# A layer with memory attention on one core: products of high and low parts for the memory's keys and values, and the keys' projection ahead of the last trunk stage

## Chip, core and metric

The kernel runs on one core of one Trainium2 chip. The metric is the device time of one execution in microseconds, the median of several runs. TensorE (PE) multiplies matrices, VectorE (DVE) and ScalarE (ACT) work on tiles, GpSimd (POOL) takes some copies, and SyncE (SP) issues the DMAs between memory and the core.

## What is computed

One layer on 2048 positions of width 1024: a mixer (dilated window attention beside a gated convolution), a cross-attention into 256 fixed memory tokens, and an MLP. Everything is float32. What the change touches is the cross-attention:

```python
def memory_cross_attention(h, mem_n, w_q_mem, w_kv_mem, w_o_mem):
    q = (h @ w_q_mem).reshape(b, s, N_MEM_HEADS, MEM_HEAD_DIM)
    kv = mem_n @ w_kv_mem
    k, v = jnp.split(kv, 2, axis=-1)
    ...
    scores = jnp.einsum('bshe,bmhe->bhsm', q, k).astype(jnp.float32) / math.sqrt(MEM_HEAD_DIM)
    p = jax.nn.softmax(scores, axis=-1).astype(v.dtype)
    o = jnp.einsum('bhsm,bmhe->bshe', p, v).reshape(b, s, D_MODEL)
    return o @ w_o_mem

x = x + hybrid_mixer(rms_norm(x, g_mix), ...)
x = x + memory_cross_attention(rms_norm(x, g_xattn), rms_norm(mem, g_mem), ...)
x = x + squared_relu_mlp(rms_norm(x, g_mlp), w_up, w_down)
return rms_norm(x, g_final)
```

The memory does not depend on x, so the kernel folds it into the weights: the keys K = mem_n @ w_k are multiplied once with w_q (per head, 256 columns), and the values V with w_o. The 2048 positions then need one product with the folded query weights and one with the folded output weights.

## The kernel before

All products of the trunk run on TensorE in *groups* of 28 *steps*. A step multiplies one tile of weights with one tile of data and is numbered through (group times 28); `step(n)` issues its products, `ahead` prepares operands of a later one, `behind` and `done` take the results out of PSUM. Groups come in this order: two groups each of "vg", "ux" and "qk" (the mixer's projection, the last one, "qk" for the second half, is steps 84 to 111), then the dilated attention, then "w" (the mixer's output projection), "s" and "o" (scores and outputs of the memory), and the MLP.

The trunk's float32 products are already taken of high and low parts: an operand x is split into hi = x rounded to the reduced type float32r (ScalarE, L205 for weights, L298 for data) and lo = x - hi (VectorE, L212 and L309), and hi·hi + hi·lo + lo·hi is accumulated in PSUM (L416, 512 columns; L411, 256 columns). The memory's four sets of products are not: `mem_proj` (L1060) for keys and values, `fold_q` (L1043) for w_q times the keys and `fold_o` (L1331) for the values times w_o are plain float32 matmuls, of 128x256, 128x256 and 128x512. Each set goes over eight weight tiles of 128x1024.

Between step 111 and the attention stands a loop of 16 turns: eight of `mem_proj` (keys, into K5), then eight of `fold_q`. In it SP is told to load the first queries (`load_q`) and keys (`load_k`, L762), VectorE copies the keys to the second 64 partitions (`dup_k`, the cast at L769), and the first two score products (`qk`, L827 and L828) stand ahead of the last `fold_q`. The last convolution block, conv(0, 0), is spread over these turns too (scaled copies on ScalarE, taps at L680 and L681 on VectorE, row sums L114 on TensorE).

The attention repeats scores, softmax, transposes and products, and its tail combines three patterns (`combine`: sums at L927 to L939 on VectorE over rows that go out to memory and back). Its end is followed by a loop of 16 turns: `mem_proj` for the values and `fold_o`, beside which the combined attention is normalised and the operands of "w" are made.

The order is written by hand: each engine executes its instructions in the order in which the program issues them, `after(n, fn)` issues fn at step n, and `later(d, fn)` d turns after the current one. An instruction that waits holds all that stand behind it on its engine. Buffers are rings: 20 pages of 128x2048 floats (`page`), six smaller ones (`w4`), eight of `s2`, eight PSUM banks; taking the next buffer makes its writer wait for the last reader of the one that had it. `Weights` loads tiles in pairs, seven ahead. DMAs from SP take eight queues in turn.

Of the kernel before, what the change touches and what calls it, by code (L numbers as in the profile page):

```python
# [50 lines left out]
def _body(tc, a, out):  # L51
# [75 lines left out]
    class Weights:  # L127
        def __init__(self, srcs):
            self.srcs, self.raw = srcs, {}
# [10 lines left out]

        def get(self, i):
            for d in range(7):
                self.load(i + d)
            return self.raw[i]
# [544 lines left out]
    for (hf, j), ds in {(0, 1): (60, 63, 66, 70), (1, 0): (85, 88, 91, 94), (1, 1): (103, 105, 107, 109),  # L689
                        (0, 0): (117, 118, 119, 121)}.items():  # L690
# [9 lines left out]
    def mk(k):  # L700
        return mem["x"][:, k]

# [16 lines left out]
    WS2 = Weights([a["w_kv"][i] for i in range(8)] + [a["w_qT"][i] for i in range(8)])  # L719
    for n, fn, *args in ((32, mem_load, a["memT"]), (40, mem_rows), (94, mem_load, memd),  # L720
                         (98, WS2.load, 0), (106, WS2.load, 2), (109, WS2.load, 4)):
        after(n, fn, *args)
    for k in range(2):
        after(34 + 2 * k, mem_sum, k)
    for k in range(KC):
        after(41 + k, mem_scale, k)
    for n in range(V0 - 4, V0):
        ahead(n)
    for n in range(V0, 4 * 28):
        step(n, n > V0)  # L730
# [299 lines left out]
    A = {}  # L1030
    K5 = page([128, KC, J])

    def fold_q(t):
# [6 lines left out]
        w = WS2.get(8 + t)  # L1040
        for fc in range(KC):
            ps = bk["f"][fc // 2][:, fc % 2 * J:fc % 2 * J + J]
            pe.matmul(ps, w[:, fc], K5[:, t], start=e == 0 and fc % 2 == 0, stop=e == 1, skip_group_check=True)  # L1043
# [13 lines left out]
    def mem_proj(t, w, KV):  # L1057
        ps = bank()[:, :J]
        for k in range(KC):
            pe.matmul(ps, w[:, k], mk(k), start=k == 0, stop=k == KC - 1)  # L1060
        act.activation(KV[:, t], ps, AF.Copy)

    for j in range(16):
        if j < 8:
            mem_proj(j, WS2.get(j), K5)
        else:
            if j == 15:
                act.activation(dummy, ones, AF.Exp)
                qk(0)
                qk(1)  # L1070
            fold_q(j - 8)
        behind(4 * 28 + j)
        if j == 4:
            load_q(0)
        if j == 10:
            load_v(0, 2)
        if j in (6, 7, 8, 9):
            load_k(0, (j - 6) // 2, (j - 6) % 2)
        if j in (10, 11, 12, 13):
            dup_k(0, (j - 10) // 2, (j - 10) % 2, dve)  # L1080
# [3 lines left out]
    for i in range(len(units) + 4):  # L1084
# [7 lines left out]
        if i == 192 - 40:  # L1092
# [8 lines left out]
            later(43, WS.load, 6)  # L1101
        tick()
# [213 lines left out]
    V5 = page([128, KC, J])  # L1316

    def fold_o(t):
# [7 lines left out]
        for jb in range(2):  # L1326
            jl = slice(jb * 128, jb * 128 + 128)
            for nh in range(2):
                ns = slice(nh * 4, nh * 4 + 4)
                ps = bk["f"][jb][nh]  # L1330
                pe.matmul(ps, V5[:, t, jl], w[:, ns], start=e == 0, stop=e == 1)  # L1331
# [176 lines left out]
```

## Time and profile before

| | us |
|---|---|
| median of 3 runs (2668.38 to 2672.39) | 2671.26 |
| the profiled execution | 2672.2 |
| its span, first to last instruction | 2670.4 |
| TensorE busy in it | 2622.3 |
| VectorE busy | 2188.5 |
| ScalarE busy | 1443.3 |
| step 111 ends, the keys' products begin | 509.07 |
| the fold of the keys begins | 538.49 |
| the attention's scores run on from | 579.49 |
| the values' products begin | 853.18 |
| the fold of the values begins | 881.68 |
| stage "w" begins | 911.29 |

The upper rows are of the whole execution, the lower ones are start times in its timeline, on TensorE. A row of the timeline has start, duration, engine, line, operation and tiles; in square brackets stands the idle time of the engine before it and what ended that. A row of groups by line has the busy time of the whole group, the mean of one in ns, and idle time. A row of windows has for its stretch the busy time of PE, PEld, DVE, ACT and POOL (with counts), then the granted TensorE clock, the DMA share and GB/s.

### The profile page before, as it was taken

How to read it: one execution, taken by the hardware profiler on the slowest of the kernel's cores; microseconds unless marked ns; L12 is line 12 of the kernel's file. 1: busy time of each engine (PE TensorE's matmuls, PEld its weight loads, DVE VectorE, ACT ScalarE, POOL GpSimd, SP SyncE). 2: the span in 40 equal slices, each digit the busy share in tenths (PEclk: the TensorE clock that was granted, in tenths of full speed). 3: DMA queues.
4: the chain of work that ended last, by engine and by line, in shares of the span. 5: the costliest groups of instructions: out<-in, count | busy, mean ns of one | idle time of the engine just before them, and what ended most of it. 6: DMA issues, size and time to landing. Idle time of an engine off the chain costs nothing.

```text
span 2670.4 us, 35198 instructions
## 1 busy us (share of the span) xinstructions
PE 2622.3 (98%) x13286; PEld 2158.6 (81%) x13286; DVE 2188.5 (82%) x3405; ACT 1443.3 (54%) x2450; POOL 144.1 (5%) x181
## 2 busy tenths in 40 slices
PE   8999999989999999999999999999999999999998
PEld 6787988878888678888888888888887888888886
DVE  6879868658777689888999877879789987978788
ACT  5445545458776234667445546474644637365563
POOL 0000000002654200000000000000000000000000
PEclk9999999999999999999999999999999999999999
DMA  5856664994778866565683211111120511111111
GB/s 191 278 178 203 213 215 154 315 250 104 162 161 250 256 224 230 186 207 228 232 299 117 85 48 64 63 63 64 63 95 32 189 63 63 64 34 57 52 48 63
DMA packets 201673, 391.67 MB, mean 147 GB/s; under 512 B 21664, under 2 KB 77344, under 8 KB 188064
## 3 DMA queue, kind: packets, MB, share of 16 engines
q1 hardware_dynamic: 200960, 388.90, 45.0%
q8 instruction: 105, 1.72, 0.3%
q14 instruction: 64, 0.52, 0.1%
q10 hardware_dynamic: 544, 0.52, 0.1%
HBM read 277.12 MB, written 112.26 MB: 146 GB/s over the span
## 4 chain that ended last, share of the span: by engine, by line
PE 81%; DVE 9%; DMA 6%; ACT 2%; issue 1%; POOL 1%; SPq 1%; DVEq 0%; POOLq 0%; ACTq 0%
PE ps L416 65%; PE ps L884 3%; PE ps L867 2%; PE ps L433 2%; PE ps L827 2%; PE ps L411 1%; DMA pg<-qkd 1%; PE ps L828 1%; DVE pg L309 1%; DVE w L212 1%; PE ps L114 1%; DMA bgd<-pg 1%; PE ps L1060 1%; PE ps L1331 1%; POOL pg L954 1%
## 5 line engine op out<-in xcount | busy, mean ns | idle before, releaser
L416 PE MATMUL ps<-pg,w 128*128 128x512 f32 x8844 | 2033.3, 391 | 10.7 <-DVE pg L309 4.9
L416 PEld LDWEIGHTS ps<-pg,w 128*128 128x128 f32 x8844 | 1655.1, 188 | 359.8 <-DVE pg L309 10.5
L205 ACT ACTIVATE w<-pg 128x1024 fp32r<-128x1024 f32 x288 | 303.4, 1053 | 283.1 <-PE ps L416 237.6
L212 DVE TENSOR_TENSOR w<-pg,w 128x1024 fp32r<-128x1024 f32 x288 | 351.8, 1222 | 57.0 <-ACT w L205 56.4
L309 DVE TENSOR_TENSOR pg<-pg 128x1024 fp32r<-128x1024 f32 x300 | 365.0, 1217 | 5.0 <-ACT pg L298 4.6
L298 ACT ACTIVATE pg<-pg 128x1024 fp32r<-128x1024 f32 x300 | 305.8, 1046 | 29.2 <-DVE pg L264 11.3
L850 ACT ACTIVATE s<-s,stat 128x256 f32<-128x256 f32 (+1 forms) x384 | 172.6, 451 | 48.8 <-DVE stat L839 47.3
L1249 DVE TENSOR_TENSOR pg<-ps,pg 128x512 f32<-128x512 f32 x223 | 152.2, 685 | 53.6 <-PE ps L416 50.5
L445 ACT ACTIVATE s<-pg 128x1024 f32<-128x1024 f32 x79 | 83.3, 1057 | 187.1 <-DVE pg L1126 105.2
L205 ACT ACTIVATE w<-s 128x1024 fp32r<-128x1024 f32 x92 | 96.9, 1053 | 123.4 <-PE ps L416 74.7
L839 DVE CUSTOM_DVE_ANT_0 s<-ps,w 128x256 f32<-128x256 f32 (+1 forms) x344 | 109.0, 371 | 32.3 <-PE ps L828 27.1
L1220 DVE TENSOR_TENSOR pg<-ps,pg 128x512 f32<-128x512 f32 x96 | 66.0, 688 | 77.6 <-PE ps L416 77.6
L264 DVE TENSOR_TENSOR pg<-pg 128x1024 f32<-128x1024 f32 x104 | 126.7, 1218 | 1.5 <-DMA pg<-ptd 0.6
L212 DVE TENSOR_TENSOR w<-s,w 128x1024 fp32r<-128x1024 f32 x92 | 111.9, 1217 | 2.5 <-ACT w L205 2.4
L827 PE MATMUL ps<-pg 128*128 128x256 f32 x384 | 108.0, 313 | 0.7 <-DVE pg L769 0.7
L870 DVE COPY s<-ps 128x256 f32<-128x256 f32 (+1 forms) x192 | 101.0, 567 | 8.7 <-ACT s L850 8.0
L1215 ACT ACTIVATE pg<-ps 128x512 f32<-128x512 f32 x96 | 56.9, 595 | 90.2 <-PE ps L416 89.6
L1221 ACT ACTIVATE pg<-pg 128x512 f32<-128x512 f32 x96 | 60.6, 631 | 80.9 <-DVE pg L1220 80.8
L309 DVE TENSOR_TENSOR pg<-s,pg 128x1024 fp32r<-128x1024 f32 x78 | 94.5, 1220 | 9.7 <-ACT pg L298 9.6
L828 PE MATMUL ps<-pg 128*128 128x256 f32 x384 | 98.2, 287 | 3.7 <-DVE pg L769 3.7
L39 DVE TENSOR_TENSOR s<-s,s 128x1024 f32<-128x1024 f32 x56 | 69.2, 1236 | 31.5 <-ACT s L445 31.5
L867 PE MATMUL ps<-ident,s 128*128 128x128 f32 x600 | 86.4, 279 | 8.8 <-ACT s L850 8.3
(159 smaller groups left out, 2484.4 us busy)
## 6 DMA issues: line engine op xcount, KB each, us to landing
pg<-w_up SPq DMA_DIRECT2D x32, 1024.0 KB
pg<-w_down SPq DMA_DIRECT2D x32, 1024.0 KB
pg<-smd SPq DMA_DIRECT2D x24, 1024.0 KB
pg<-xT SPq DMA_DIRECT2D x19, 1024.0 KB
pg<-w_in SPq DMA_DIRECT2D x18, 1024.0 KB
qkd<-pg SPq DMA_DIRECT2D x64, 256.0 KB
pg<-qkd SPq DMA_DIRECT2D x32, 512.0 KB
pg<-x2d SPq DMA_DIRECT2D x16, 1024.0 KB
```

The costliest lines, as they stand in the source:

```text
L205: act.activation(hi, src, AF.Copy)
L212: dve.tensor_tensor(lo, src, f(hi), OP.subtract)
L264: dve.tensor_tensor(to, x, y, op)
L298: act.activation(hi, src, AF.Copy)
L309: dve.tensor_tensor(lo, src, f(hi), OP.subtract)
L416: pe.matmul(ps, wt[l][:, m % 2, k * 128:k * 128 + 128], o[x][:, k, cols], start=k == 0 and j == 0 and p in (1, 2, 5), stop=k == 3 and j == ...
L827: pe.matmul(Sh, qv, kv[0], start=True, stop=False)
L828: pe.matmul(Sh, qv, kv[1], start=False, stop=True)
L839: dve.tensor_tensor_reduce(smv, sv, mv, -0.125, 3e38, OP.add, OP.min, mt[:, c1:c1 + 1])
L850: act.activation(pout, pin, AF.Exp, bias=mt[:, c1:c1 + 1], scale=-1.0, accum_out=zt[:, c1:c1 + 1])
L867: pe.transpose(pt[:, j * 256 + h * 128:j * 256 + h * 128 + 128], PR[i][:, h * 256 + half * 128:h * 256 + half * 128 + 128], ident)
L1249: dve.tensor_tensor(y, ps, y, OP.add)
```

## The change

`Weights` gets a method `split` that makes a high and a low part of a tile, in two halves of a page or (pages=False) in two `w4` buffers; `get` splits one tile ahead and returns the pair. The memory is split the same way in four instructions (`mem_split`). The keys and values are taken from PSUM as a high copy (ScalarE) and a low part (VectorE). Every product of `mem_proj`, `fold_q` and `fold_o` becomes three, of PARTS. The keys' projection goes out of the loop behind step 111 to a place between steps 83 and 84, with its loads at steps 68 to 80 instead of 98 to 109; the loop behind step 111 keeps the eight turns of `fold_q`. The taps of conv(0, 0) go from steps 117 to 121 to 112 to 116, and the loads of queries and keys to turns 0 and 1.

```diff
+        def split(self, i):
+            if i >= len(self.srcs) or i in self.hl:
+                return
+            w = self.raw[i]
+            if self.pages:
+                t = page([128, 2, KC, 128], F32R)
+                hi, lo = t[:, 0], t[:, 1]
+            else:
+                hi, lo = (w4([128, KC, 128], F32R) for l in range(2))
+            act.activation(hi, w, AF.Copy)
+            later(1, dve.tensor_tensor, lo, w, f(hi), OP.subtract)
+            self.hl[i] = hi, lo
+
         def get(self, i):
             for d in range(7):
                 self.load(i + d)
-            return self.raw[i]
+            for d in range(2):
+                self.split(i + d)
+            return self.hl[i]
...
-                        (0, 0): (117, 118, 119, 121)}.items():
+                        (0, 0): (112, 113, 115, 116)}.items():
...
+    def mem_split(k, part):
+        c = slice(4 * k, 4 * k + 4)
+        if k == part == 0:
+            mem["hl"] = [page([128, KC, J], F32R) for l in range(2)]
+        hi, lo = (t_[:, c] for t_ in mem["hl"])
+        if part == 0:
+            act.activation(hi, mem["x"][:, c], AF.Copy)
+        else:
+            dve.tensor_tensor(lo, mem["x"][:, c], f(hi), OP.subtract)
...
-    WS2 = Weights([a["w_kv"][i] for i in range(8)] + [a["w_qT"][i] for i in range(8)])
-    for n, fn, *args in ((32, mem_load, a["memT"]), (40, mem_rows), (94, mem_load, memd),
-                         (98, WS2.load, 0), (106, WS2.load, 2), (109, WS2.load, 4)):
+    WS2 = Weights([a["w_kv"][i] for i in range(8)])
+    WS3 = Weights([a["w_qT"][i] for i in range(8)], False)
+    for n, fn, *args in ((32, mem_load, a["memT"]), (40, mem_rows), (66, mem_load, memd),
+                         (68, WS2.load, 0), (72, WS2.load, 2), (80, WS2.load, 4),
+                         (100, WS3.load, 0), (104, WS3.load, 2), (107, WS3.load, 4), (109, WS3.load, 6),
+                         (72, mem_split, 0, 0), (73, mem_split, 0, 1), (74, mem_split, 1, 0), (75, mem_split, 1, 1),
+                         (80, WS2.split, 0), (81, WS2.split, 1), (108, WS3.split, 0), (109, WS3.split, 1)):
...
+    PARTS = ((0, 0), (0, 1), (1, 0))
+    K5 = []
+
+    def mem_proj(t, w, KV):
+        ps = bank()[:, :J]
+        if t == 0:
+            KV.extend(page([128, KC, J], F32R) for l in range(2))
+        for k in range(KC):
+            for j, (l, x) in enumerate(PARTS):
+                pe.matmul(ps, w[l][:, k], mem["hl"][x][:, k], start=k == j == 0, stop=k == KC - 1 and j == 2)
+        act.activation(KV[0][:, t], ps, AF.Copy)
+        later(1, dve.tensor_tensor, KV[1][:, t], ps, f(KV[0][:, t]), OP.subtract)
+
     for n in range(V0, 4 * 28):
-        step(n, n > V0)
+        if n == 3 * 28:
+            done(n - 1)
+            for j in range(8):
+                mem_proj(j, WS2.get(j), K5)
+                tick()
+        step(n, n != V0 and n != 3 * 28)
...
-        w = WS2.get(8 + t)
+        w = WS3.get(t)
         for fc in range(KC):
             ps = bk["f"][fc // 2][:, fc % 2 * J:fc % 2 * J + J]
-            pe.matmul(ps, w[:, fc], K5[:, t], start=e == 0 and fc % 2 == 0, stop=e == 1, skip_group_check=True)
+            for j, (l, x) in enumerate(PARTS):
+                pe.matmul(ps, w[l][:, fc], K5[x][:, t], start=e == 0 and fc % 2 == 0 and j == 0, stop=e == 1 and j == 2,
+                          skip_group_check=True)
...
-    for j in range(16):
-        if j < 8:
-            mem_proj(j, WS2.get(j), K5)
-        else:
-            if j == 15:
-                act.activation(dummy, ones, AF.Exp)
-                qk(0)
-                qk(1)
-            fold_q(j - 8)
+    for j in range(8):
+        if j == 7:
+            act.activation(dummy, ones, AF.Exp)
+            qk(0)
+            qk(1)
+        fold_q(j)
         behind(4 * 28 + j)
-        if j == 4:
+        if j == 0:
             load_q(0)
-        if j == 10:
+        if j in (0, 1):
+            for i in range(2):
+                load_k(0, j, i)
+        if j == 2:
             load_v(0, 2)
-        if j in (6, 7, 8, 9):
-            load_k(0, (j - 6) // 2, (j - 6) % 2)
-        if j in (10, 11, 12, 13):
-            dup_k(0, (j - 10) // 2, (j - 10) % 2, dve)
+        if j in (4, 5):
+            for i in range(2):
+                dup_k(0, j - 4, i, dve)
         tick()
...
+            for k in range(2):
+                later(36 + k, mem_split, k, 0)
+                later(37 + k, mem_split, k, 1)
+                later(39 + k, WS.split, k)
...
-                pe.matmul(ps, V5[:, t, jl], w[:, ns], start=e == 0, stop=e == 1)
+                for j, (l, x) in enumerate(PARTS):
+                    pe.matmul(ps, V5[x][:, t, jl], w[l][:, ns], start=e == 0 and j == 0, stop=e == 1 and j == 2)
```

What this does to the order of an engine is shown at three places. The line numbers of the changed code are higher, by 17 at L416, which becomes L433; the splits of weights are L152 (high) and L39 (low, as every operation issued through `later`), the memory's products L769, their high copies L770, the fold's products L1092 and its copies L1100 and L1102, the key casts L820, the score products L878 and L879.

ScalarE behind the last copy of group 2, before the change. w4 are high parts of trunk weights, pg_3384 of data, and L667 scales the convolution.

```order
L205 ACTIVATE w4_3381<-pg_3274 128x1024 [waits DVE_49,DMAHW5_49,PE_49,Activation_49]
L298 ACTIVATE pg_3384<-pg_1553 128x1024 [waits DMAHW3_49]
L636 ACTIVATE pg_3400<-ps_3387 128x512 [waits PE_49]
L298 ACTIVATE pg_3384<-pg_1553 128x1024
L667 ACTIVATE pg_3418<-pg_2835,conv_w_152 128x512
L636 ACTIVATE pg_3400<-ps_3405 128x512 [waits PE_49]
```

And of the change, where the keys' projection now stands: pg_3365, pg_3436, pg_3466 and pg_3496 take the parts of the weights 1 to 4, pg_3408 the high part of the keys.

```order
L152 ACTIVATE pg_3365<-pg_3089 128x1024 [waits DMAHW4_49,PE_49]
L222 ACTIVATE w4_3370<-pg_3215 128x1024
L770 ACTIVATE pg_3408<-ps_3407 128x256 [waits DVE_49,PE_49]
L152 ACTIVATE pg_3436<-pg_3171 128x1024 [waits DMAHW6_49,DVE_49]
L770 ACTIVATE pg_3408<-ps_3438 128x256
L152 ACTIVATE pg_3466<-pg_3171 128x1024 [waits DMAHW7_49,DVE_49,PE_49]
L770 ACTIVATE pg_3408<-ps_3468 128x256
L152 ACTIVATE pg_3496<-pg_3343 128x1024 [waits DMAHW4_49,DVE_49]
```

The copies of the trunk's step 84 have gone behind, and the keys' high copies stand in turn with the splits of the next weights, each of which waits for VectorE and, at two places, TensorE.

VectorE between step 111 and the attention, before: convolution taps (L680, L681), the fold's copies (L1052) and the key casts (L769).

```order
L1052 TENSOR_SCALAR pg<-ps,g_xattn 128x256 x4
L680 SCALAR_TENSOR_TENSOR pg<-pg,conv_w 128x384
L681 SCALAR_TENSOR_TENSOR pg<-s_3998,conv_w,pg 128x128
L769 CAST pg<-pg 64x2048
L680 SCALAR_TENSOR_TENSOR pg<-pg,conv_w 128x256
L681 SCALAR_TENSOR_TENSOR pg<-s_3998,conv_w,pg 128x256
L39 TENSOR_TENSOR pg<-pg 128x1024
L1052 TENSOR_SCALAR pg<-ps,g_xattn 128x256 x4
L769 CAST pg<-pg 64x2048 x2
L39 TENSOR_TENSOR s_4172<-s_4172,s_4234 128x1024
L1052 TENSOR_SCALAR pg<-ps,g_xattn 128x256 x4
L769 CAST pg<-pg 64x2048
```

The same place of the change, from the copies of tiles 2 and 3 on: w_4418 and w_4465 are low parts of the weights 4 and 5 of w_qT.

```order
L1102 TENSOR_SCALAR pg<-ps,g_xattn 128x256 x4
L39 TENSOR_TENSOR w_4418<-pg,w_4417 128x1024
L697 SCALAR_TENSOR_TENSOR pg<-pg,conv_w 128x384
L698 SCALAR_TENSOR_TENSOR pg<-s_4269,conv_w,pg 128x128
L820 CAST pg<-pg 64x2048 x2
L697 SCALAR_TENSOR_TENSOR pg<-pg,conv_w 128x256
L698 SCALAR_TENSOR_TENSOR pg<-s_4269,conv_w,pg 128x256
L39 TENSOR_TENSOR w_4465<-pg,w_4464 128x1024
L697 SCALAR_TENSOR_TENSOR pg<-pg,conv_w 128x384
L698 SCALAR_TENSOR_TENSOR pg<-s_4269,conv_w,pg 128x128
L1102 TENSOR_SCALAR pg<-ps,g_xattn 128x256 x4
L820 CAST pg<-pg 64x2048 x2
```

The low parts stand behind the copies of the tile before and, for weight 5, behind the casts of the first two keys; the casts of the other two stand ahead of weight 6's.

SP from the last weights of w_kv to the attention's first loads, before (qkd holds queries and keys, w_kv and w_qT weights):

```order
L139 DMA pg<-w_kv 128x1024 x2
L455 DMA qkd<-pg 128x512 x4
L139 DMA pg<-w_qT 128x1024 x4
L740 DMA pg<-qkd 64x2048 x4
L139 DMA pg<-w_qT 128x1024 x2
L762 DMA pg<-qkd 64x2048 x2
L139 DMA pg<-w_qT 128x1024 x2
L762 DMA pg<-qkd 64x2048 x2
L773 DMA pg<-vd 128x16x128
```

And of the change:

```order
L140 DMA pg<-w_qT 128x1024 x2
L472 DMA qkd<-pg 128x512 x4
L472 DMA cvd<-pg 128x4x512
L472 DMA qkd<-pg 128x512 x2
L828 DMA w_4283<-masks 128x640
L791 DMA pg<-qkd 64x2048 x4
L813 DMA pg<-qkd 64x2048 x2
L472 DMA qkd<-pg 128x512 x2
L813 DMA pg<-qkd 64x2048 x2
L472 DMA qkd<-pg 128x512 x2
L824 DMA pg<-vd 128x16x128
```

The weights have left the place between the stores and the loads of queries and keys; two pairs of stores of the last block stand between the key loads.

13 lines of the change are left out of this document (4 added, 9 removed).

## The prediction

> **What bounds the kernel now.** I read the page's busy times and chain first, then the groups by line with shapes kept apart.
>
> ```profile
> span 2670.4 us, 35198 instructions
> PE 2622.3 (98%) x13286; PEld 2158.6 (81%) x13286; DVE 2188.5 (82%) x3405; ACT 1443.3 (54%) x2450; POOL 144.1 (5%) x181
> PE 81%; DVE 9%; DMA 6%; ACT 2%; issue 1%; POOL 1%; SPq 1%; DVEq 0%; POOLq 0%; ACTq 0%
> ```
>
> TensorE is busy 98% of the span and carries 81% of the chain that ended last, so a matmul saved is worth its time, as long as nothing else becomes late there. The products that the change touches are L1060 (keys, values), L1043 (the fold of the keys into the query weights) and L1331 (the fold of the values into the output weights); L411 and L416 show what a high/low product costs at the two widths.
>
> ```profile
> L416 PE MATMUL ps<-pg,w 128*128 128x512 f32 x8820 | 2030.0, 391 | 9.3 <-DVE pg L309 4.9 <-ACT pg L298 2.9 <-DVE pg L1220 1.2
> L411 PE MATMUL ps<-w,pg 128*128 128x256 f32 x576 | 73.2, 287 | 0.6 <-DVE w L212 0.6
> L1060 PE MATMUL ps<-pg 128*128 128x256 f32 x256 | 56.2, 379 | 0.0
> L1331 PE MATMUL ps<-pg 128*128 128x512 f32 x64 | 27.9, 593 | 0.0
> L205 ACT ACTIVATE w<-pg 128x1024 fp32r<-128x1024 f32 x288 | 303.4, 1053 | 283.1 <-PE ps L416 237.6 <-DMA pg<-w_in 11.5 <-PE ps L411 9.6
> L212 DVE TENSOR_TENSOR w<-pg,w 128x1024 fp32r<-128x1024 f32 x288 | 351.8, 1222 | 57.0 <-ACT w L205 56.4
> ```
>
> The mean in a row is latency; the busy sum over the count is what one costs in a row of them. L416: 2030.0/8820 = 0.230 us. L411: 73.2/576 = 0.127. A plain float32 product has two records, so L1060 is 56.2/128 = 0.44 each and L1331 27.9/32 = 0.87. L205 and L212 are the making of a high and a low part of one 128x1024 weight tile: 1.05 us on ScalarE, then 1.22 on VectorE.
>
> The stage between the last trunk step and the attention is next, TensorE and windows.
>
> ```profile
> 509.07 20.88 PE L1060 MATMUL ps<-pg 128*128 128x256 f32 x96
> 538.49 20.88 PE L1043 MATMUL ps<-pg 128*128 128x256 f32 x96
> 562.15 5.08 PE L1043 MATMUL ps<-pg 128*128 128x256 f32 x16 [2.78 <-DMA pg<-w_qT]
> 572.25 0.58 PE L828 MATMUL ps<-pg 128*128 128x256 f32 x1 [3.70 <-DVE pg L769]
> 577.79 1.84 PE L114 MATMUL ps<-ones,s 128*128 128x1 f32 x16
> 579.49 0.36 PE L827 MATMUL ps<-pg 128*128 128x256 f32 x1
> ```
>
> ```profile
> 431.00:509.00 78.00, 78.00 (x354) 64.84 (x353) 69.30 (x94) 45.27 (x58) 0.00 (x0) 1.00 0.67 225
> 509.00:538.00 29.00, 29.00 (x144) 25.73 (x143) 9.44 (x25) 5.85 (x12) 0.00 (x0) 1.00 1.04 323
> 538.00:580.00 42.00, 34.81 (x160) 30.06 (x159) 20.30 (x40) 14.74 (x33) 5.95 (x8) 0.92 1.00 234
> 560.00:564.00 4.00, 1.85 (x5) 1.53 (x6) 1.11 (x1) 2.33 (x5) 1.58 (x2) 0.69 1.10 176
> 572.00:576.00 4.00, 3.75 (x13) 3.31 (x14) 1.22 (x9) 2.34 (x10) 0.00 (x0) 0.60 1.03 403
> ```
>
> Call T = 509.07 the end of step 111. The attention runs steadily from 579.49, so the stage takes **70.4 us**. In it TensorE computes the keys (some 28 us) while the DMA share is 1.04; later it waits 2.78 us for a weight and 3.70 for a key cast. Each wait leaves a stretch of lower clock: 0.69 and 0.60 in the last two windows, after a clock of 1.00 before.
>
> **The products themselves.** Three passes replace one plain product. Keys and values: 64 products each of 0.44 become 192 of 0.127, 28.1 to 24.4 us, -3.7 each. The fold of the keys has the same shape and count: 28.1 to 24.4, -3.7. Fold of the values: 32 of 0.87 become 96 of 0.230, 27.9 to 22.1, -5.8. Together **-16.9 us** of TensorE time, if every operand is there.
>
> The Trainium skill ("FP8 and Floating Point Precision", section "TensorE Precision Notes") says that true float32 takes four passes of high and low parts. By that rule and the 0.127, the plain product would be 0.51 and the saving on the three narrow groups 24.4 us rather than 11.1, an estimate from that page; the row says 0.44, so 3.5 passes, and the sum goes by the row.
>
> **What the splits add, and where.** Each of the 32 weight tiles now needs a high part (1.05, ScalarE) and a low part (1.22, VectorE). A tile lasts 24 x 0.127 = 3.05 us on TensorE, 2.76 in the fold of the values. So the engines have time; the question is what stands ahead in their queues, since a split is made only one tile ahead.
>
> *Keys between steps 83 and 84.* The order of ScalarE shows that the first high copy of the keys (L770) waits for the end of tile 1's products, and that the high part of weight 2 behind it waits for a VectorE product of the finished stage. These are the rows that VectorE must do there first.
>
> ```profile
> 431.27 0.69 DVE L606 TENSOR_TENSOR pg<-ps,pg 128x512 f32<-128x512 f32 x1 [0.47 <-PE ps L416]
> 431.99 1.23 DVE L609 TENSOR_TENSOR pg<-pg 128x1024 f32<-128x1024 f32 x1
> 433.14 1.22 DVE L212 TENSOR_TENSOR w<-pg,w 128x1024 fp32r<-128x1024 f32 x1
> ```
>
> Step 83 ends near 431 (call it s). After s VectorE has one low part of the weight, three such 0.69, two 1.23 and three more of 1.22 (low parts of step 84 among them): 1.22 + 2.07 + 2.46 + 3.66 = 9.4, less their overlap of about 0.09 each, some 8.7. Then hi (1.05) and lo (1.22): tile 2 starts at s+10.9 instead of s+6.1, a stall of 4.8. Weight 3's high part needs the pages of tile 2, so it waits for its end: 0.38 + 1.05 + 1.22 less overlap, a stall of 2.1. From there pages are free. End: 24.4 + 6.9 = **s+31.3**. Lower bound 24.4 (nothing waits), upper 24.4 + 8 x 2.3 = 42.8 (every tile waits for its pair); I take 31.3 since the queue shows two waits.
>
> *The fold, now right at T.* It had 28 us of key products ahead of it, under which the query and key loads ran. Three rows of the SP queue and the VectorE rows that wait for them:
>
> ```profile
> 526.54 3.08 SPq L740 DMA_DIRECT2D pg<-qkd  x4
> 534.77 2.94 SPq L762 DMA_DIRECT2D pg<-qkd  x2
> 544.13 2.57 SPq L762 DMA_DIRECT2D pg<-qkd  x2
> 511.71 1.22 DVE L39 TENSOR_TENSOR s<-s,s 128x1024 f32<-128x1024 f32 x1
> 531.67 0.16 DVE L99 TENSOR_SCALAR tmp<-ps 128x4 f32<-128x4 f32 x1 [17.53 <-PE ps L114]
> 532.99 0.62 DVE L680 SCALAR_TENSOR_TENSOR pg<-pg,conv_w 128x384 f32<-128x384 f32 x1
> 534.19 0.48 DVE L681 SCALAR_TENSOR_TENSOR pg<-s,conv_w,pg 128x256 f32<-128x256 f32 x1
> 543.87 0.88 DVE L1052 TENSOR_SCALAR pg<-ps,g_xattn 128x256 f32<-128x256 f32 x2 [2.48 <-PE ps L1043]
> 554.84 1.22 DVE L769 CAST pg<-pg 64x2048 fp32r<-64x2048 f32 x1 [7.03 <-DMA pg<-qkd]
> 566.90 1.22 DVE L769 CAST pg<-pg 64x2048 fp32r<-64x2048 f32 x1 [5.79 <-DMA pg<-qkd]
> ```
>
> Before, keys arrive at T+45.8 and T+57.8 behind 5 MB of weights that now load earlier. The eight query and key loads are 4.2 MB. They can't start before step 111's stores land, T+6 to T+13 (12 stores and a mask); at the 176 to 234 GB/s of 560:564 and 538:580 they take 18 to 24 us. So key 2 is in at about **T+27.3** and key 4 at T+33 to 36, some 20 us earlier than before against T, but the fold now starts 29.4 us earlier (538.49 - 509.07).
>
> VectorE's queue then sets the low parts. Weight 2's stands behind step 111's tail (3.9 after T in the row at 511.71, one more such, and 2.3 for the splits added in steps 108 and 109, so 7.3), a conv tap pair (0.62 + 0.35, as at 532.99), the four evictions of tile 1 (1.76), another pair (0.96) and itself, each less its overlap: T+11.9, and TensorE, done with tile 1 at T+6.1, stalls 5.8. Weight 3's comes at 15.8 (0.8), weight 4's, behind four evictions, at 20.7 (1.9). Tile 4 ends at 23.7. Weight 5's stands behind the casts of keys 1 and 2: 27.3 + 1.22 + 0.96 + 1.13 (a 1.22 less overlap) = 30.6, a stall of 6.9. Tile 5 ends at 33.7, its evictions at 35.4, keys 3 and 4 cast by 37.3, then the small rows of the row norm (1.3, from 531.67 to 532.99), a tap pair, a 1.22 sum and the low part: T+41, a stall of 5.5 beside the 1.84 of row sums (577.79). Then tile 6 (3.05), the first eight score products (1.9, at 0.24; the one at 572.25 took 0.58 with its latency), tile 7 (3.05): T+49.1. With the second row sums inside, the attention is steady at about **T+49.5**, bounds T+42 (key 4 at 36, one cast, then scores, tile 7 and rows) and T+55 (the loads at T+33 slipping by 6, as in the 5.79 above).
>
> Keys and fold: 31.3 + 49.5 = 80.8 against 70.4: **+10.4**.
>
> *Clock.* Windows 560:564 and 572:576 show the price of a stall of 2.8 or 3.7 us: a stretch near half clock, some 3.4 us long, so 1.7 us lost. Of the four new stalls above 4 us, that of the keys and those ahead of tiles 5 and 6 are on the path: **+5.1**, bounds 0 and 13.6 (four of twice that length). The Trainium skill ("TensorE: Matmul & The Clock Gate", section "🔬 Part 1: The HAM clock gate (the "warmup" mystery)") has a free-running window of about 3.4 us whose outcome depends on where it falls; by it each of the six stalls above 2.9 us may cost nothing or 1.7, and the sum below would lie between +7 and +18. The two windows of this trace agree with the half speed.
>
> *Values and their fold.* In the attention's tail and after it:
>
> ```profile
> 860.52 0.19 DVE L927 TENSOR_TENSOR w<-w 128x32 f32<-128x32 f32 x1 [6.71 <-DMA w<-mzd]
> 864.46 0.27 ACT L932 ACTIVATE w<-w 128x96 f32<-128x96 f32 x1
> 876.76 1.29 DVE L39 TENSOR_TENSOR pg<-pg,w 128x512 f32<-128x512 f32 x2 [5.31 <-DMA w<-btd]
> 881.68 20.76 PE L1331 MATMUL ps<-pg 128*128 128x512 f32 x48
> 911.29 2.99 PE L416 MATMUL ps<-pg,w 128*128 128x512 f32 x12
> 916.62 3.54 PE L114 MATMUL ps<-ones,s 128*128 128x1 f32 x16 [2.33 <-DVE s L39]
> 850.00:914.00 64.00, 64.00 (x276) 44.34 (x274) 31.07 (x57) 18.81 (x33) 8.77 (x7) 1.00 0.80 249
> ```
>
> Here VectorE has 33 of 64 us free, so 16 low parts (18 us) and eight of 0.48 fit, but the low part of weight 2 stands behind the sum at L927, which waits for a DMA until 860.5: ready near 863.1 against 860.1, a stall of 3.0; weight 3's stands behind the parts that follow the exponent of 864.46: 3.5. The rest has room. So -9.5 + 6.5 + 1.7 (one clock stretch) = **-1.3**, bounds -9.5 (no stall) and +6 (both stalls doubled, and the tail's 2.33 twice).
>
> *What is moved and hidden.* The memory's own splits (two of 1.05 and 1.22 in steps 72 to 75, two in the attention) lie beside TensorE: VectorE is busy 69.3 of 78 us in 431:509, ScalarE 45.3. The loads of the memory and the key weights go up from steps 94 to 109 to steps 66 to 80 and those of w_qT from behind T to steps 100 to 109, ahead of as many stores in SP's queue; that window has a DMA share of 0.67, and as many bytes as leave it come in. I cost both at nothing; without cover the splits are 4 x 2.3 = 9 us, and 4 MB at 225 GB/s 19 us.
>
> **Sum.** 10.4 + 5.1 - 1.3 = +14.2 against the profiled execution, 2672.2 us, which has 1.8 around its span and lies 0.9 above the median of 2671.26: 2671.26 + 14.2 = 2685.5.
>
> **Rivals.**
> 1. *The products decide (faster).* All low parts are ready a tile ahead and the loads are in before the scores: -16.9, and the 0.7 + 3.7 of waits for keys go too: 2650 to 2654. It decides if VectorE's low part comes less than 3.05 us after the last. For it: VectorE is free for 33 of 64 us in the values. Against it: the fixed order behind two DMA waits in both folds.
> 2. *Only the loads bind.* The queue order costs nothing, key 4 does: T+42 and s+24.4 give 66.4, -4.0; with -9.5 of the values and a clock stretch of 1.7, -11.8: 2659.
> 3. *The stalls are half of what I count, without clock loss.* 27.9 + 45 = 72.9, +2.5, values -6: within 0.2%, 2668.
> 4. *High/low at the plain rate* would add 0.31 x 576 = 180 us; L411, the same form and width, excludes it.
>
> **How the numbers follow.** Forecast 0.68 (own range 2677 to 2697), rival 1 0.07, rival 2 0.11, rival 3 0.14. The clock's upper bound and T+55 reach 2700; below, the range goes to 2660, where rival 2 begins. Faster by over 0.2% (below 2666, about what can be told from no change): rivals 1 and 2 and a little of 3, 0.20; within: 0.12; slower: 0.68.
>
> **What would show it.** Right: L769 in the new code stalls at tiles 2 and 3 between the steps; the fold's L1092 with waits of about 5 us ahead of tiles 2, 5 and 6, ended by VectorE's low parts; PEclk below 1 there; the values' products with two waits of some 3 us, then none. Wrong: no idle ahead of tile 2 (the tiles' pages were free earlier than the order implies), or key casts that end before T+27, or L1092's waits ended by the DMA alone.

## The result, and the profile after

| | before | after |
|---|---|---|
| median, us | 2671.54 (4 runs, 2668.38 to 2672.39) | 2715.85 (4 runs, 2712.53 to 2718.26) |
| ratio | | 1.0167 (95%: 1.0155 to 1.0179) |
| profiled execution / its span | 2672.2 / 2670.4 | 2718.26 / 2716.0 |

The kernel is slower by 44.3 us, three times the 14.2 that were forecast, and beyond the range. The page of the changed kernel: span, busy times, chain.

```profile
span 2716.0 us, 35743 instructions
PE 2627.5 (97%) x13510; PEld 2181.1 (80%) x13510; DVE 2236.8 (82%) x3457; ACT 1477.2 (54%) x2486; POOL 144.4 (5%) x181
PE 81%; DVE 9%; DMA 5%; ACT 2%; issue 1%; POOL 1%; SPq 1%; DVEq 0%; POOLq 0%; ACTq 0%
```

The shares hardly move; they are no help. TensorE is busy 5 us longer, where the prediction had 16.9 us less. The groups of the three products, by line and shape (busy, mean of one, idle ahead and what ended it), tell more:

```profile
L769 PE MATMUL ps<-pg 128*128 128x256 f32 x384 | 60.2, 326 | 14.0 <-DVE pg L39 8.5 <-ACT pg L152 5.5
L1092 PE MATMUL ps<-pg,w 128*128 128x256 f32 x192 | 31.3, 332 | 20.5 <-DVE w L39 18.7 <-ACT w L152 1.8
L1379 PE MATMUL ps<-pg 128*128 128x512 f32 x96 | 28.2, 455 | 12.6 <-DVE pg L39 12.6
```

At 0.127 and 0.230 each they would take 48.8, 24.4 and 22.1 us: 95.3 in place of 119.7. The idle time ahead of them is 47.1 us, ended by splits (L39 low, L152 high). Before, the idle time ahead of the same groups was 2.8. The keys and their fold in the timeline of TensorE:

```profile
429.95 5.91 PE L769 MATMUL ps<-pg 128*128 128x256 f32 x48
440.20 0.54 PE L769 MATMUL ps<-pg 128*128 128x256 f32 x2 [4.34 <-ACT pg L152]
441.46 5.06 PE L769 MATMUL ps<-pg 128*128 128x256 f32 x22 [0.72 <-DVE pg L39]
447.66 0.79 PE L769 MATMUL ps<-pg 128*128 128x256 f32 x2 [1.15 <-ACT pg L152]
448.92 16.71 PE L769 MATMUL ps<-pg 128*128 128x256 f32 x118 [0.47 <-DVE pg L39]
465.48 4.72 PE L433 MATMUL ps<-pg,w 128*128 128x512 f32 x20
543.51 5.91 PE L1092 MATMUL ps<-pg,w 128*128 128x256 f32 x48
551.20 0.51 PE L1092 MATMUL ps<-pg,w 128*128 128x256 f32 x2 [1.77 <-ACT w L152]
555.18 8.12 PE L1092 MATMUL ps<-pg,w 128*128 128x256 f32 x48 [3.48 <-DVE w L39]
565.17 3.14 PE L1092 MATMUL ps<-pg,w 128*128 128x256 f32 x24 [1.87 <-DVE w L39]
575.30 5.07 PE L1092 MATMUL ps<-pg,w 128*128 128x256 f32 x22 [6.99 <-DVE w L39]
588.85 5.06 PE L1092 MATMUL ps<-pg,w 128*128 128x256 f32 x22 [6.34 <-DVE w L39]
594.84 3.04 PE L1092 MATMUL ps<-pg,w 128*128 128x256 f32 x24
```

A tile of 24 products takes 3.04 us where the clock is full (594.84), and 22 of them take 5.06 behind a wait. The first two products of a tile need only its high part, so most waits stand two products into a tile. The values and their fold:

```profile
877.36 7.50 PE L769 MATMUL ps<-pg 128*128 128x256 f32 x48
887.37 4.63 PE L769 MATMUL ps<-pg 128*128 128x256 f32 x24 [1.84 <-DVE pg L39]
895.76 5.06 PE L769 MATMUL ps<-pg 128*128 128x256 f32 x22 [3.76 <-DVE pg L39]
903.55 13.02 PE L769 MATMUL ps<-pg 128*128 128x256 f32 x94 [1.74 <-DVE pg L39]
918.28 5.74 PE L1379 MATMUL ps<-pg 128*128 128x512 f32 x24 [1.25 <-DVE pg L39]
926.69 5.73 PE L1379 MATMUL ps<-pg 128*128 128x512 f32 x24 [2.67 <-DVE pg L39]
936.66 7.88 PE L1379 MATMUL ps<-pg 128*128 128x512 f32 x22 [4.24 <-DVE pg L39]
951.21 7.50 PE L1379 MATMUL ps<-pg 128*128 128x512 f32 x22 [4.40 <-DVE pg L39]
958.90 3.00 PE L433 MATMUL ps<-pg,w 128*128 128x512 f32 x12
```

And the windows of the three places; the number behind the engines is the granted clock, then DMA share and GB/s:

```profile
430.00:466.00 36.00, 29.33 (x196) 28.21 (x195) 18.94 (x22) 10.80 (x17) 0.00 (x0) 0.81 0.15 59
544.00:600.00 56.00, 35.54 (x234) 34.51 (x232) 38.20 (x72) 22.26 (x42) 7.49 (x8) 0.76 0.99 286
877.00:959.00 82.00, 62.10 (x325) 54.71 (x321) 48.66 (x73) 31.50 (x44) 12.94 (x10) 0.81 0.63 180
```

By stages the span's 45.6 us come out so. Steps 84 to 111 take 78.0 in both.

| stage | before | after | measured | forecast |
|---|---|---|---|---|
| keys ahead of step 84 | 0 | 465.48 - 429.95 = 35.5 | | |
| step 111 to tile 7's end and one set of row sums | 70.4 | 597.72 + 1.84 - 543.51 = 56.05 | +21.2 with the row above | +15.5 |
| rest of the attention | 853.2 - 579.5 = 273.7 | 877.4 - 599.6 = 277.8 | +4.1 | 0 |
| values and their fold | 911.3 - 853.2 = 58.1 | 958.9 - 877.4 = 81.5 | +23.4 | -1.3 |
| all else | | | -3.1 | 0 |

Of the +23.4, the values' projection has 10.5 (39.0 us, 877.36 to 916.40, against 28.5) and their fold 12.9 (42.5 against 29.6).

### The profile page after: what moved, and what is told of

It reads as the page before. It is cut to its first block, busy times and chain, and to the rows that moved or that the text cites. A ratio compares the mean times of both kernels' runs of the same rounds, so it can differ in the third digit from the quotient of the medians.

```text
span 2716.0 us, 35743 instructions
## 1 busy us (share of the span) xinstructions
PE 2627.5 (97%) x13510; PEld 2181.1 (80%) x13510; DVE 2236.8 (82%) x3457; ACT 1477.2 (54%) x2486; POOL 144.4 (5%) x181
## 3 DMA queue, kind: packets, MB, share of 16 engines
q8 instruction: 106, 1.74, 0.3%
## 4 chain that ended last, share of the span: by engine, by line
PE 81%; DVE 9%; DMA 5%; ACT 2%; issue 1%; POOL 1%; SPq 1%; DVEq 0%; POOLq 0%; ACTq 0%
PE ps L433 65%; PE ps L935 2%; PE ps L450 2%; PE ps L918 2%; PE ps L878 2%; PE ps L428 2%; PE ps L769 1%; PE ps L879 1%; DMA vd<-pg 1%; PE ps L114 1%; DVE pg L326 1%; DVE w L229 1%; PE ps L1379 1%; POOL pg L1005 1%; DMA pg<-qkd 1%
## 5 line engine op out<-in xcount | busy, mean ns | idle before, releaser
L433 PE MATMUL ps<-pg,w 128*128 128x512 f32 x8844 | 2033.0, 390 | 9.6 <-DVE pg L326 5.9
L433 PEld LDWEIGHTS ps<-pg,w 128*128 128x128 f32 x8844 | 1654.7, 188 | 358.4 <-DVE pg L326 12.0
L901 ACT ACTIVATE s<-s,stat 128x256 f32<-128x256 f32 (+1 forms) x384 | 172.5, 451 | 44.3 <-DVE stat L890 43.0
L890 DVE CUSTOM_DVE_ANT_0 s<-ps,w 128x256 f32<-128x256 f32 (+1 forms) x344 | 108.9, 370 | 32.8 <-PE ps L879 28.1
L1267 DVE TENSOR_TENSOR pg<-ps,pg 128x512 f32<-128x512 f32 x96 | 65.9, 687 | 77.6 <-PE ps L433 77.6
L878 PE MATMUL ps<-pg 128*128 128x256 f32 x384 | 107.3, 311 | 0.0
L1268 ACT ACTIVATE pg<-pg 128x512 f32<-128x512 f32 x96 | 60.6, 631 | 80.9 <-DVE pg L1267 80.8
L879 PE MATMUL ps<-pg 128*128 128x256 f32 x384 | 97.5, 286 | 0.0
L315 ACT ACTIVATE pg<-s 128x1024 fp32r<-128x1024 f32 x78 | 82.0, 1052 | 22.6 <-DVE s L281 22.4
```

Source lines behind the costliest of these rows:

```text
L315: act.activation(hi, src, AF.Copy)
L433: pe.matmul(ps, wt[l][:, m % 2, k * 128:k * 128 + 128], o[x][:, k, cols], start=k == 0 and j == 0 and p in (1, 2, 5), stop=k == 3 and j == ...
L878: pe.matmul(Sh, qv, kv[0], start=True, stop=False)
L879: pe.matmul(Sh, qv, kv[1], start=False, stop=True)
L890: dve.tensor_tensor_reduce(smv, sv, mv, -0.125, 3e38, OP.add, OP.min, mt[:, c1:c1 + 1])
L901: act.activation(pout, pin, AF.Exp, bias=mt[:, c1:c1 + 1], scale=-1.0, accum_out=zt[:, c1:c1 + 1])
```

## The experiments

Each of these runs has a ratio to runs of the kernel before made beside it, whose medians go from 2667.16 to 2670.45 us. A difference between the microseconds of two such runs is therefore good to a few us only; the stages of the profiles are the surer measure.

**The values plain again.** Everything of the change stays but the values' products and their splits (those of the memory at the attention's end too).

```diff
-            mem_proj(t, WS.get(t), V5)
+            mem_plain(t, WS.get_raw(t), V5)
...
-                for j, (l, x) in enumerate(PARTS):
-                    pe.matmul(ps, V5[x][:, t, jl], w[l][:, ns], start=e == 0 and j == 0, stop=e == 1 and j == 2)
+                pe.matmul(ps, V5[0][:, t, jl], w[:, ns], start=e == 0, stop=e == 1)
...
```

> The values' projection and fold are plain float32 products again, as before the change; the keys' part stays as changed. Theory A: the loss of the values' part, 877.4 to 958.9 against 853.2 to 911.3 (23.4 us), goes; 2690 to 2695 us, with the keys' part unchanged. Rival: the attention's tail comes late whatever the products are (its sums go to memory and back); then less than 8 us go, 2708 or more.

Measured 2691.9 us (2 runs; 1.0083 of before, 1.0057 to 1.0108). The values' part goes from 873.10 to 931.22, 58.1 us as before. So half of the loss is made there, and by the products of high and low parts with their splits.

**The move alone.** All products plain, no splits; the keys' projection, the loads and the taps where the change has them.

```diff
-                mem_proj(j, WS2.get(j), K5)
+                mem_plain(j, WS2.get_raw(j), K5)
...
-        w = WS3.get(t)
+        w = WS3.get_raw(t)
...
-            for j, (l, x) in enumerate(PARTS):
-                pe.matmul(ps, w[l][:, fc], K5[x][:, t], start=e == 0 and fc % 2 == 0 and j == 0, stop=e == 1 and j == 2,
-                          skip_group_check=True)
+            pe.matmul(ps, w[:, fc], K5[0][:, t], start=e == 0 and fc % 2 == 0, stop=e == 1, skip_group_check=True)
...
```

> Only the move: keys' projection between steps 83 and 84, loads and convolution taps as in the change, but every product plain float32 and no splits. Theory A: the move itself costs little; keys 28.1 plus a fold that ends with the key casts near 42 us after step 111 give 70 against 70.4: 2668 to 2676 us, with one wait for keys ahead of the scores. Rival B (transfers, uncovered by the move): the fold's stage stays near the 54 us of the change; 2680 or more.

Measured 2672.57 us (8 runs; 1.0007, 0.9994 to 1.0019): no difference. Its timeline, TensorE and the key casts (L832) on VectorE; its fold began at 537.21:

```profile
559.63 3.70 PE L1103 MATMUL ps<-pg 128*128 128x256 f32 x16
568.75 0.58 PE L890 MATMUL ps<-pg 128*128 128x256 f32 x1 [5.43 <-DMA pg<-qkd]
574.01 4.52 PE L1103 MATMUL ps<-pg 128*128 128x256 f32 x16
```

```profile
565.00 1.22 DVE L832 CAST pg<-pg 64x2048 fp32r<-64x2048 f32 x1 [0.93 <-DMA pg<-qkd]
571.50 1.22 DVE L832 CAST pg<-pg 64x2048 fp32r<-64x2048 f32 x1 [0.76 <-DMA pg<-qkd]
```

Keys 2 and 4 are cast from 27.8 and 34.3 us after step 111, where the prediction had 27.3 and 33 to 36. The move's own cost is this: ahead of the first scores TensorE waits for key loads that the projection used to cover, and it gives back what the earlier projection took off the stage: the projection takes 27.4 us (431.56 to 459.00) and the rest 42.8 (counted as in the table), 70.2 together against 70.4.

**High/low products without the move.** The loop of 16 turns, its loads and taps are those of before; every product is of high and low parts. The parts of the keys' weights lie in the small buffers (`w4`), and the memory is split at steps 100 to 103.

```diff
-        if n == 3 * 28:
-            done(n - 1)
-            for j in range(8):
-                mem_proj(j, WS2.get(j), K5)
-                tick()
-        step(n, n != V0 and n != 3 * 28)
+        step(n, n > V0)
...
```

> Only the high/low products: keys' projection back behind step 111, with the loop, loads and taps of before, the splits added (low parts a turn later, in the small buffers). Theory A: the values' part keeps its 23 us of loss, the keys' part of the stage still waits for low parts, less than 20 us in all as the loads are covered; 2695 to 2715 us. Rival B: the loss came with the move; then the keys' stage gains the 7 us of products, and the whole is 2688 or less.

Measured 2706.08 us (2 runs; 1.0136, 1.011 to 1.0162). That is 36.0 us above the kernel before measured beside it, where the change has 44.3, so most of the loss is that of the products, wherever the keys stand.

**Low parts at once.** One edit: the order of the low part on VectorE.

```diff
             act.activation(hi, w, AF.Copy)
-            later(1, dve.tensor_tensor, lo, w, f(hi), OP.subtract)
+            dve.tensor_tensor(lo, w, f(hi), OP.subtract)
```

> The only edit: the low part of a weight is issued in the turn that issues its high part, not a turn later, so on VectorE it stands ahead of the fold's copies of the tile that runs meanwhile. Theory A (order): the waits of TensorE for VectorE's low parts (18.7 us ahead of the keys' fold, 12.6 ahead of the values' fold, 8.5 ahead of the projections) come mostly from that order, and the half clock behind them falls with them. The values' fold should lose its waits ahead of tiles 2, 4 and 6 (from 42 to about 25 us from its first product to stage w), the keys' fold its waits ahead of tiles 4 and 5; 2680 to 2692 us. Rival B (transfers): the low parts are late because key loads and the combined sums come late; then at most 5 us are saved, 2711 to 2716.

Measured 2698.4 us (4 runs; 1.01, 1.0077 to 1.0123), 17.5 less than the change (16.0, each against the kernel before measured beside it) and 6 more than hoped. What the old order did can be read off VectorE in the changed kernel, in the fold of the values:

```profile
922.24 0.69 DVE L1385 COPY pg<-ps 128x512 f32<-128x512 f32 x1 [1.95 <-PE ps L1379]
923.60 0.69 DVE L1385 COPY pg<-ps 128x512 f32<-128x512 f32 x1 [0.67 <-PE ps L1379]
924.21 1.28 DVE L39 TENSOR_TENSOR pg<-pg,w 128x512 f32<-128x512 f32 x2
925.41 2.96 DVE L39 TENSOR_TENSOR pg<-pg 128x1024 fp32r<-128x1024 f32 x3
```

The low part of tile 2 (the first of the last row, it ends at 926.6) stands behind the copies of tile 1 (L1385), which wait for tile 1's last products, and behind sums that were queued in the same turn. TensorE ends tile 1 at 924.02 and waits 2.67 us for it. The same order stands ahead of every second tile, so no free VectorE time can cover these waits.

With the low part at once, the projection of the values takes 25.3 us (874.21 to 899.52), against 39.0 in the change and 28.5 in the kernel before, and the fold of the keys 47.4 in place of 54.2. The fold of the values hardly gains: 40.6 us (to 940.11) in place of 42.5, where some 25 were expected. Its waits ahead of tiles 0, 2 and 4 are gone, but others stand ahead of tiles 1, 3, 5, 6 and 7, 9.3 us in all, where the change has 12.6. Those of tiles 3, 6 and 7:

```profile
911.42 6.88 PE L1379 MATMUL ps<-pg 128*128 128x512 f32 x22 [2.18 <-DVE pg L153]
926.58 1.22 PE L1379 MATMUL ps<-pg 128*128 128x512 f32 x2 [2.44 <-ACT pg L152]
935.78 4.13 PE L1379 MATMUL ps<-pg 128*128 128x512 f32 x10 [2.16 <-DVE pg L153]
```

So the order made the waits of the changed kernel, but mending it hardly shortens that fold: the parts then come late for other reasons. The low part for tile 3 stands behind a sum that waits 2.14 us for a DMA, and the high part for tile 6 starts on ScalarE only at 925.47, after 5.91 us of idle time whose cause the profile doesn't show. The whole part of the values is 65.9 us in place of 81.5. The attention takes some of the gain back: it is 3.0 us longer, 277.6 in place of 274.6 from its second row sums. The keys' projection stays at 35.5, since its longer waits are for high parts (4.34 and 1.15), which this edit doesn't move.

**TensorE kept busy while it waits.** No order on another engine changes.

```diff
+    def fill(ps, n):
+        for _ in range(n):
+            pe.matmul(ps[:, :128], ident, ident, start=True, stop=True, skip_group_check=True)
...
+        fill(ps, ({2: 18, 3: 8} if KV is K5 else {2: 8, 3: 15, 4: 8}).get(t, 0))
```

and the same ahead of eight tiles of the two folds.

> The changed kernel with small plain products of the identity (128x128, some 0.2 us each, results overwritten) put on TensorE where it waits: 8 to 28 ahead of tiles 2 to 6 of the keys, their fold, the values and their fold, as many as the waits last. No order on another engine changes. Theory C (clock): the half clock after a wait costs time of its own; kept busy, TensorE stays at full clock, the products of L769, L1092 and L1379 (60.2, 31.3, 28.2 us busy) come near 49, 25 and 23 and the time falls by 8 to 18 us, to 2698 to 2708. Theory A (waits alone): what is late is VectorE's low parts, which do not hang on the clock; 2713 to 2720.

Measured 2706.04 us (4 runs; 1.0143, 1.0119 to 1.0167), 9.8 less (7.4, each against the kernel before measured beside it), although TensorE does 191 small products more. The intervals of the two ratios overlap a little, so the trace is the better evidence. Groups and windows of this run (L775, L1101 and L1391 are the three products):

```profile
L775 PE MATMUL ps<-pg 128*128 128x256 f32 x384 | 49.8, 289 | 2.5 <-DVE pg L39 2.2 <-ACT pg L152 0.3
L1101 PE MATMUL ps<-pg,w 128*128 128x256 f32 x192 | 25.6, 287 | 3.6 <-DVE w L39 3.6
L1391 PE MATMUL ps<-pg 128*128 128x512 f32 x96 | 24.9, 409 | 2.6 <-DVE pg L39 2.6
```

```profile
430.00:461.00 31.00, 29.54 (x245) 28.94 (x244) 18.75 (x22) 10.44 (x15) 0.00 (x0) 1.00 0.18 69
539.00:590.00 51.00, 47.36 (x400) 46.35 (x399) 38.07 (x72) 22.62 (x42) 6.20 (x8) 1.00 1.02 297
871.00:948.00 77.00, 73.34 (x478) 67.17 (x477) 48.76 (x72) 30.90 (x44) 14.24 (x10) 0.92 0.64 188
```

The clock is 1.00 in place of 0.81 and 0.76 at the keys and their fold, 0.92 in place of 0.81 at the values, and the products take 100.3 us in place of 119.7. The keys' projection lasts 31.1 us (429.75 to 460.83) in place of 35.5, their fold 49.4 from step 111 to tile 7's end (538.86 to 588.28) in place of 54.2, and the values' projection 34.3 (870.71 to 905.05) in place of 39.0. The fold of the values isn't shorter, 43.0 us against 42.5, though its products are (24.9 busy in place of 28.2): what it saves on products it waits for the parts.

**Both together.** Low parts at once, and the fill where that run still waited.

> The run with low parts at once and, at the places where it still waits, the small identity products that keep TensorE's clock up (keys tiles 2 and 3, their fold 2, 6 and 7, values' fold 1, 3, 5, 6 and 7). Theory C (clock): what the order left of the half clock goes as well, 6 to 11 us, to 2687 to 2692. If clock and order are the same loss counted twice: 2696 to 2699.

Measured 2688.55 us (4 runs; 1.0087, 1.0066 to 1.0109), 9.9 below the order alone (6.9, each against the kernel before measured beside it), and all four runs lie below 2696. In the profiles the keys' projection is 4.5 us shorter than with the order alone (31.1), their fold 2.8 (44.7) and the values' part 3.1, so the gain of the clock comes on top of that of the order. The values' part is 62.8 us (865.02 to 927.85), still 4.7 above that of before, with products at 49.2, 25.4 and 23.9 us.

**What still stretches the values' fold: transfers?** On top of low parts at once:

```diff
+                if i >= 10:
+                    self.raw[i + j] = self.raw[8 + j]
+                    sp.dma_start(t[:, j, 0, 0:16], self.srcs[i + j][:, 0:16])
+                    continue
...
```

> The run with low parts at once, and six of the eight tiles of w_o (3 MB) not loaded: their products take the first two tiles' data in their place, so the values' fold isn't the reference's. All splits and products are there. Theory D (transfers bind the values' fold once the order is mended; DMA share 1.02 to 1.06 from 898 to 922): the part from the values' first product to stage w falls from 65.9 to 52 to 57 us, the whole to 2684 to 2690. Rival (splits and copies on ScalarE and VectorE bind it): 64 us or more, 2695 to 2699.

Measured 2695.53 us (2 runs; 1.0101, 1.0073 to 1.013). The values' part is 64.0 us (872.08 to 936.12) against 65.9, and its fold 38.2 against 40.6, so the 3 MB of loads bind little of it. The theory of transfers fell.

**Or GpSimd?** Again on top of low parts at once:

```diff
+        if pr == 3 and eng is pool:
+            return
...
```

> The run with low parts at once, without the combined sums that GpSimd takes beside the values' fold (the last two blocks of 512 positions of the last head pair keep one pattern's unweighted values, so the output isn't the reference's). In the run with low parts at once a low part took 2.3 us on VectorE in 929 to 938 while GpSimd ran, 1.22 elsewhere. Theory E (VectorE and GpSimd slow each other): low parts and conversions stay at 1.22, the values' part falls from 65.9 to 58 to 62 us, the whole to 2690 to 2695. Rival: something else stretches them, or they aren't late for TensorE; 65 us, 2697 to 2699.

Measured 2690.77 us (2 runs; 1.0087, 1.0067 to 1.0108). The part takes 60.6 us (871.74 to 932.37), 5.3 less, and its fold 34.5 in place of 40.6. Last low part of the fold, first in the run with low parts at once, then in this one:

```profile
933.44 2.29 DVE L153 TENSOR_TENSOR pg<-pg 128x1024 fp32r<-128x1024 f32 x1
```

```profile
926.02 1.22 DVE L153 TENSOR_TENSOR pg<-pg 128x1024 fp32r<-128x1024 f32 x1
```

GpSimd's sums in the run with low parts at once, one while VectorE was idle and one beside that low part:

```profile
925.17 1.26 POOL L39 TENSOR_TENSOR pg<-pg 128x512 f32<-128x512 f32 x1
```

```profile
934.72 2.15 POOL L39 TENSOR_TENSOR pg<-pg 128x512 f32<-128x512 f32 x1
```

In these rows each takes 1.7 to 1.9 times as long beside the other. Not both always do: a sum that had begun first, at 926.40, took 1.27 us while the low part at 926.56 took 2.19. The Trainium skill ("SBUF — State Buffer", section "Who interferes with whom") states that a VectorE instruction with two SBUF inputs contends with a GpSimd instruction that reads SBUF, over a pair of ports that the two engines share and that it calls an exclusive lock; these rows agree, as 2.29 is not far below 2.48, the sum of 1.22 and 1.26.

What is left of the fold's loss in this run, 4.9 us over the 29.6 of before, isn't explained by any run. Of its 5.6 us of waits, 4.1 are now for high parts (2.94 of them at 925.91).

**Only what gained: the values' projection.** The kernel before, with high and low parts for that projection alone, low parts at once.

```diff
-            mem_proj(t, WS.get(t), V5)
+            mem_proj_hl(t, WS.get_hl(t), V5)
...
```

> The kernel before, with one part of the change only: the values' projection of high and low parts, low parts issued with the high ones; keys, both folds and all loads as before. The products should give back 3.7 us and no wait is seen there in the run with low parts at once (two of 0.8): 2666 to 2668 against 2670, faster by 0.1 to 0.15%. Rival: the stage behind it (fold of the values) is bound by transfers, 1.01 of the DMA in 882 to 911 before, so an earlier end of the projection waits there; 2670 to 2672.

Measured 2675.86 us (12 runs; 1.0027, 1.0015 to 1.0038): slower, neither theory. In its profiled execution (span 2671.0) the values' part does take less, 856.08 to 911.62, 55.5 us. But it starts 2.9 us later, and this row of the attention's end says why:

```profile
854.49 1.35 PE L913 MATMUL ps<-s,pg 128*64 128x128 f32 x16 [2.85 <-DVE s L899]
```

The low parts of the first two weights, which themselves wait 1.40 us for ScalarE, stand in VectorE's queue ahead of a copy (L899) of the last unit. Stage "w" begins 0.3 us later than before (911.62 against 911.29), so this profile doesn't place the 6.7 us between the medians (2675.86 and 2669.17); the runs of this kernel spread from 2670.5 to 2682.2, and the profiled one, 2672.8, is among the faster.

**Only the keys, where they were.** High and low parts for the keys and their fold, in the place of before, low parts at once, values plain; the edits are those of the first, third and fourth run together (values plain, no move, low parts at once).

> High/low products for the keys and their fold alone, in the place and with the loads of the kernel before, low parts issued with the high ones; the values plain. If the order was all that stood against them, TensorE has 7.4 us less to do from 509 to 579, and the keys' loads, which landed at 554.8 and 566.9 before, become the bound: the stage takes 65 to 69 us against 70.4 and the whole 2664 to 2669 against some 2669. If the lower parts still come late behind key casts that wait for loads (as in the run without the move, 84.5 us for the stage), 72 us or more and 2671 to 2680.

Measured 2675.3 us (11 runs; 1.0018, 1.0009 to 1.0028). The rival holds. The stage lasts 508.5 to 584.8, 76.3 us, with this row in it:

```profile
564.36 8.35 PE L1098 MATMUL ps<-pg,w 128*128 128x256 f32 x48 [8.48 <-DVE w L153]
```

and on VectorE of the same run the cast that waits, and the low part that stands behind it and three short operations:

```profile
559.77 1.22 DVE L826 CAST pg<-pg 64x2048 fp32r<-64x2048 f32 x1 [7.09 <-DMA pg<-qkd]
563.09 1.22 DVE L153 TENSOR_TENSOR w<-pg,w 128x1024 fp32r<-128x1024 f32 x1
```

No version tried is faster than the kernel before. Splits queued two tiles ahead were not tried.

## Why the prediction failed, by its own steps

The span grew by 45.6 us, 31.4 more than the 14.2 of the sum. By the table, 24.7 of this is in the values and their fold, 5.7 in the keys and theirs with the clock, 4.1 in the attention, and -3.1 elsewhere.

**What bounds the kernel** was right: the stages between the trunk's groups, with VectorE's queue and the key loads as the limits. The direction came out of it.

**Keys between steps 83 and 84** was right as a mechanism: a wait ahead of tile 2 (4.34 + 0.72, forecast 4.8) and of tile 3 (1.15 + 0.47, forecast 2.1). At full clock the stage is 31.1 us, forecast 31.3.

**The fold at T** likewise: waits ahead of tiles 2, 4, 5 and 6 of 5.3, 1.9, 7.0 and 6.3 against 5.8, 1.9, 6.9 and 5.5 (the 0.8 ahead of tile 3 didn't come). The cast of key 2 waits for its load until 571.98, 28.5 us after step 111, and weight 5's low part stands behind it, as forecast (27.3):

```profile
571.98 1.22 DVE L820 CAST pg<-pg 64x2048 fp32r<-64x2048 f32 x1 [1.15 <-DMA pg<-qkd]
574.03 1.22 DVE L39 TENSOR_TENSOR w<-pg,w 128x1024 fp32r<-128x1024 f32 x1
```

Tile 7 ends 49.4 us after step 111 at full clock, forecast 49.1.

**Clock** was mis-sized. The prediction priced a stretch of low clock at 1.7 us and counted three on the path of the keys and their fold, 5.1, and one at the values. Measured against the filled run, keys and fold lose 35.5 - 31.1 = 4.4 and 54.2 - 49.4 = 4.8, so 9.2, and the values' projection 39.0 - 34.3 = 4.7. Two reasons show in the rows. A stretch can cost more: 48 products at 555.18 took 8.12, 2 us more than at full clock, behind a wait of 3.5. And low clock came behind waits of 1.84 and 1.74 at the values as well (24 products in 4.63, 94 in 13.02, where 3.0 and 11.9 are due), though not behind each: 24 products behind 1.87, at 565.17, took 3.14. The prediction left short waits out. The Trainium skill ("TensorE: Matmul & The Clock Gate", section "HAM oscillation — how this bites in real kernels") warns of idle gaps above some 3.4 us; here shorter ones, several in a row, did it too, and the measurement decides.

**Values and their fold** is the step that failed. The two waits in the projection were right as a mechanism, and a third was left out (6.5 forecast; measured 1.84 + 3.76 + 1.74 = 7.3). The projection still took 39.0 us where 28.5 - 3.7 + 6.5 + 1.7 = 33.0 were forecast; most of the difference is low clock. Then the prediction said "The rest has room", which put the waits of the fold at nothing: 29.6 - 5.8 = 23.8 us. The fold took 42.5. Waits ahead of tiles 0, 2, 4 and 6 make 12.6 us of the difference, and products at low clock 6.1 (28.2 us busy in place of 22.1; 22 products in 7.88 and 7.50, where 5.1 are due). "Room" was judged by VectorE's free time in 850 to 914, which is no test: ahead of tiles 2, 4 and 6 the low part of the next tile is queued behind the copies of the running one, the same order that the prediction had seen in the fold of the keys, and had not looked for here.

How much each cause is worth is shown in part. The run with low parts at once takes 15.6 of the part's 23.4 us away, but 13.7 of them in the projection and only 1.9 in the fold; without GpSimd's sums beside VectorE the fold loses a further 6.1. The last 4.9 us of the fold stay open. The bound of +6 came from doubling the two waits that were seen, so it could not hold waits in the fold.

**What is moved and hidden**: right for the loads (the move alone changes nothing that can be told) and for the memory's splits in steps 72 to 75 (step 83 ends at 429.95, near 431 in the kernel before). Wrong for the splits at the attention's end, costed at nothing: the attention is 4.1 us longer, and 272.4 (600.67 to 873.10, from the second row sums) in the run with plain values against 274.6 (602.73 to 877.36) is 2.2 less, which fits them. The other 1.9 isn't explained by any run.

**The rivals**: the products never decided, and the loads alone did not bind. The range's upper end of 2700 was made of the stage of the keys; no rival let the values' fold lose.

## What to carry to other kernels

Ask for each instruction that feeds the bottleneck what stands ahead of it on its own engine and whether that waits for the bottleneck's current work; if so, there is a wait in every turn, however idle the engine looks. Free time of an engine over a stretch doesn't show that each of its results is there in time. Splitting an operand to save, by the forecast, 13 to 21% of a short matmul (3.7 of 28.1 us, 5.8 of 27.9) paid in no version here, even with the split queued earlier. And price a wait on TensorE at more than its length: beside the 47 us of waiting, the products took 24.4 us longer than at full clock, and filling the waits took some 7 to 10 us off the whole.

## What the runs showed that was not expected

Useless products put into the waits made the kernel faster: 191 of them took some 7 to 10 us off, and the granted clock rose from 0.81 and 0.76 to 1.00 at the keys and their fold. VectorE's subtraction of two tiles takes 2.3 us in place of 1.22 while GpSimd adds tiles, and GpSimd's sums 2.15 in place of 1.26; the kernel before shows it too, 2.10 and 2.28 at 914.38 and 916.40, the first of them inside the wait of 2.33 that ends at 916.62.
